# Expert lists built from two-byte one-hots, one decode for all heads, and attention products on array halves

## The chip, the cores and the metric

The kernel runs on one core of a Trainium2 chip. The core has a matrix engine (PE, whose weight loads are shown apart as PEld), a vector engine (DVE), an activation engine (ACT), a general engine (POOL) that here issues the gathers, and SP, which issues most other DMAs. The metric is the device time of one execution in microseconds (us). Before the change it is 3013.2 us, the median of three runs (3012.96 to 3013.81).

## The reference, cut to what matters

Two transformer blocks over 256 tokens of width 2048, all in float32. The first has a windowed grouped-query attention beside a linear recurrence, then a layer of 16,384 experts (`peer`); the second has two more attentions and a gated feed-forward. The change touches three places:

```python
# first block, attention: 16 query heads of 64, 4 key heads, a sink per head
s = jnp.einsum('bnqgrd,bnkgd->bngrqk', qb, kb) * (HEAD_DIM ** -0.5)
p = jnp.exp(s - m); p = p / (jnp.sum(p, -1, keepdims=True) + jnp.exp(sk - m))
o = jnp.einsum('bngrqk,bnkgd->bnqgrd', p, vb)

# peer: per token and head, 16 best of 128 row scores, 16 best of 128 column
# scores, then the 16 best of their 256 sums
v1, i1 = lax.top_k(s1, 16); v2, i2 = lax.top_k(s2, 16)
cand = (v1[..., :, None] + v2[..., None, :]).reshape(T, 8, 256)
cidx = (i1[..., :, None] * 128 + i2[..., None, :]).reshape(T, 8, 256)
sc, sel = lax.top_k(cand, 16)
eidx = jnp.take_along_axis(cidx, sel, axis=-1); gates = softmax(sc)
# per token: sum over its 128 picks of gate * gelu(x . u_emb[e]) * v_emb[e]

# second block, dense attention of 8 heads: 128 plain and 64 rotated columns,
# the rotated key shared by the heads
s = (einsum('bqhd,bkhd->bhqk', q_nope, k_nope)
     + einsum('bqhd,bkd->bhqk', q_rope, k_rope)) * scale
```

## The kernel before

Each dense product (`linear`) splits a 1 MB weight tile into a rounded part `whi` (ACT, L123) and a rest `wlo` (DVE, L124), and runs three products per 128x512 piece (PE, L134 to L136) for the two halves of the tokens, 24 for each tile. `whi` and `wlo` rotate over four half-tiles.

The expert layer goes in four steps. Scores come from `w_pq`. The *u phase* multiplies all 16,384 expert rows `u` (32 column groups, L113 loads them, L786 applies gelu, L797 writes the activations to a DRAM table `ag`). Beside it, at a lower priority, DVE finds and decodes the picks: `top16`, the 256 sums `cand` (L605), and per head three operations that turn a pick's place into a row and a column key (L626, L628, L630). Then the gates are spread over the experts by one-hot products (L658 to L674, PE L668), 64 steps in four groups; each group is written out to `ag` (L678) and reduced (L679) to a map of the experts in use. From the map, the *list* gives each used expert a lane and a block: 16 steps of eight columns, each with one-hots of the lane (`ln`, L744) and of the block (`b1`, L746; weighted in L749 on ACT and L750 on DVE) and eight 128x202 products that add up the list of expert numbers (PE, L753). Its end (L755 to L763) gives the index tiles `idv` and `idg`. The *v phase* then gathers rows of `v_emb` (tiles `raw` and `vraw`) and of `ag` (tile `vag`) by these indices (POOL, L130) and multiplies only the blocks that are used, 12 or 24 products each; L827 to L831 make the gated activations `vh`, `vhh` and `vhl`.

The first attention (`attn1`, eight units of four heads and 128 queries) has scores with 64 rows each (L444), queries and keys lying in the lower or upper 64 partitions as the head is even or odd; `softmax_out` transposes the probabilities (L423) and multiplies with the values (L429), two heads giving the lower and two the upper 64 output partitions. In the second block's dense attention each score is a 128-row product (L1110) and a 64-row one (L1111) into one bank.

All instructions are written in program order with priorities; a scheduler sets the order on each engine before the run, and each engine then runs its own queue in that order (PE, DVE, ACT, POOL, SP each one).

Of the kernel before, what the change touches and what calls it, by code (L numbers as in the profile page):

```python
# [12 lines left out]
F32 = mybir.dt.float32  # L13
# [8 lines left out]
P = 128  # L22
T = 256
# [33 lines left out]
def tile_kernel(ctx: ExitStack, tc: tile.TileContext, A, out):  # L57
# [354 lines left out]

    def softmax_out(s, l, nh, vget, oget):

        r = small([P, nh], f"smr{nh}")
        V.reciprocal(r, l)
        for h in range(nh):
            V.tensor_scalar(s[:, h, :], s[:, h, :], r[:, h:h + 1], None, op0=ALU.mult)
        for h in range(0, nh, 2):
            tp = bank("tp")  # L420
            for hh in range(2):
                for kk in range(2):
                    TE.transpose(tp[:, (2 * hh + kk) * P:(2 * hh + kk + 1) * P],  # L423
                                 s[:, h + hh, kk * P:(kk + 1) * P], ident)
            pT = mix[0].tile([P, 4, P], F32, tag="pT", name="pT", bufs=2)
            S.activation(pT, tp.rearrange("p (a t) -> p a t", a=4), AF.Copy)
            for hh in range(2):
                for kk in range(2):
                    TE.matmul(oget(h + hh), lhsT=vget(h + hh, kk), rhs=pT[:, 2 * hh + kk, :],  # L429
                              start=kk == 0, stop=kk == 1)  # L430

# [3 lines left out]
    def attn1(c, f, tt, qT):  # L435
# [3 lines left out]
        s = ap_.tile([P, 4, T], F32, tag="s1", name="s1", bufs=3)  # L439
        for e in range(2):  # L440
            ps = bank("sc")
            b = slice(e * 64, e * 64 + 64)
            for j in range(2):
                TE.matmul(ps[:, j * T:(j + 1) * T], lhsT=qT[b, 2 * f + j, tt * P:(tt + 1) * P],  # L444
                          rhs=kT[b, g, :], start=True, stop=True)
            V.tensor_tensor(s[:, 2 * e:2 * e + 2, :], ps.rearrange("p (a t) -> p a t", a=2),
                            maskb[:, tt, :].unsqueeze(1).to_broadcast([P, 2, T]), op=ALU.add)
# [6 lines left out]
        for h in range(4):  # L454
# [6 lines left out]
        softmax_out(s, l, 4, lambda h, kk: vsb[:, kk, g * 64:g * 64 + 64],  # L461
                    lambda h: ob[h // 2 * 64:h // 2 * 64 + 64, h % 2 * P:(h % 2 + 1) * P])
        sq = sqt()
# [130 lines left out]
    for tt in range(2):  # L594
# [6 lines left out]
        sc = rt.tile([P, 8, 16], F32, tag="rsc", name="rsc")  # L601
        sel = rt.tile([P, 8, 16], U32, tag="sel", name="sel")
        for h in range(8):
            cand = rt.tile([P, 16, 16], F32, tag="cand", name="cand", bufs=2)
            V.tensor_tensor(cand, v16[:, 2 * h, :].unsqueeze(2).to_broadcast([P, 16, 16]),  # L605
                            v16[:, 2 * h + 1, :].unsqueeze(1).to_broadcast([P, 16, 16]), op=ALU.add)
            top16(sc[:, h, :], sel[:, h, :], cand.rearrange("p a b -> p (a b)"), 256)

# [9 lines left out]
        for half, op, c in ((0, ALU.logical_shift_right, 4), (1, ALU.bitwise_and, 15)):  # L618
            ai = rt.tile([P, 8, 16], U32, tag="seli", name="seli", bufs=2)
            V.tensor_scalar(ai, sel, c, None, op0=op)  # L620
            af = rt.tile([P, 8, 16], F32, tag="self", name="self", bufs=2)
            V.tensor_copy(af, ai)
            kf = rt.tile([P, 8, 16], F32, tag=f"kf{half}", name="kf")
            for h in range(8):
                eq = rt.tile([P, 16, 16], F32, tag="eq", name="eq", bufs=2)
                V.tensor_tensor(eq, af[:, h, :].unsqueeze(2).to_broadcast([P, 16, 16]),  # L626
                                iota[:, 0:16].unsqueeze(1).to_broadcast([P, 16, 16]), op=ALU.is_equal)
                V.tensor_tensor(eq, eq, xf[:, 2 * h + half, :].unsqueeze(1).to_broadcast([P, 16, 16]),  # L628
                                op=ALU.mult)
                V.tensor_reduce(kf[:, h, :], eq, axis=AX.X, op=ALU.add)  # L630
            dec.append(kf)
# [20 lines left out]
    for c in range(4):  # L652
        gsb = gp.tile([P, P, 64], F32, tag="gsb", name="gsb", bufs=1)
        for t0 in range(0, 64, 4):
            t = 64 * c + t0
            io = iota.unsqueeze(1).to_broadcast([P, 4, P])
            oh = gp.tile([P, 4, P], F32R, tag="oh2", name="oh2", bufs=2)
            V.tensor_tensor(oh, io, i2T[:, t:t + 4].unsqueeze(2).to_broadcast([P, 4, P]), op=ALU.is_equal)  # L658
            o1 = gp.tile([P, 4, P], F32, tag="oh1", name="oh1", bufs=2)
            V.tensor_tensor(o1, io, i1T[:, t:t + 4].unsqueeze(2).to_broadcast([P, 4, P]), op=ALU.is_equal)  # L660
            og = gp.tile([P, 4, 2, P], F32R, tag="og", name="og", bufs=2)
            V.tensor_tensor(og[:, :, 1, :], o1, gT[:, t:t + 4].unsqueeze(2).to_broadcast([P, 4, P]), op=ALU.mult)
# [29 lines left out]
    V.tensor_copy(trib, tri)  # L692
    iota1 = kp.tile([P, P], F32, tag="iota1", name="iota1")
    V.tensor_scalar(iota1, iota, 1.0, None, op0=ALU.add)
# [36 lines left out]
    V.tensor_scalar(ti[:, 1:2, :], pli, 7, None, op0=ALU.logical_shift_right)  # L731
    lb = kt_("lb", 2)
    V.tensor_copy(lb, ti)
    lane, blk = lb[:, 0, :], lb[:, 1, :]

    ids2 = bank("x")[:, 0:2 * NL].rearrange("p (m b) -> p m b", m=2)
    J = 8

    def bc(x, j, n):
        return x[:, j:j + J].unsqueeze(2).to_broadcast([P, J, n])  # L740

    for j in range(0, P, J):
        ln = kp.tile([P, J, P], BF16, tag="ln", name="ln", bufs=2)
        V.tensor_tensor(ln, iota.unsqueeze(1).to_broadcast([P, J, P]), bc(lane, j, P), op=ALU.is_equal)  # L744
        b1 = kp.tile([P, J, NL], BF16, tag="b1", name="b1", bufs=2)
        V.tensor_tensor(b1, iota[:, 0:NL].unsqueeze(1).to_broadcast([P, J, NL]), bc(blk, j, NL), op=ALU.is_equal)  # L746
        bb = kp.tile([P, 2, J, NL], BF16, tag="bb2", name="bb2", bufs=2)
        with prompt():
            S.activation(bb[:, 0], b1, AF.Copy, scale=pidx[:, 0:1])  # L749
        V.tensor_tensor(bb[:, 1], b1, bc(iota1, j, NL), op=ALU.mult)  # L750
        with prompt():
            for i in range(J):
                TE.matmul(ids2, lhsT=ln[:, i, :], rhs=bb[:, :, i, :], start=j + i == 0, stop=j + i == P - 1)  # L753
    ids = kp.tile([P, 2, NL], F32, tag="ids", name="ids")
# [310 lines left out]
    kr = headnorm([kb[:, 0:64], kb[:, P:P + 64]], 1, 64, r12)  # L1065
    krT = mq.tile([P, 1, T], F32, tag="krT", name="krT")
    krd = []
    for tt in range(2):
# [4 lines left out]
        krd.append(k2)  # L1073
    trans(lambda tt, j: krd[tt].rearrange("p a d -> p (a d)"), 1, krT)

    gate(0)
# [21 lines left out]
    for h0 in (0, 4):  # L1098
        for tt in range(2):
# [4 lines left out]
            for e in range(2):  # L1104
                ps = bank("sc")
                b = slice(64 * e, 64 * e + 64)
# [174 lines left out]
```

## Time and profile before

| What | Value |
|---|---|
| Median of three runs | 3013.2 us |
| Profiled execution, its own time | 3017.87 us |
| Span of its trace, first to last instruction | 3016.0 us |
| PE busy | 2958.9 us, 98% |
| DVE busy | 2005.1 us, 66% |
| ACT busy | 1578.3 us, 52% |
| Mean granted PE clock | 0.993 |

Matmuls overlap each other in the engine, so one lasts 0.39 us in the trace while the next starts 0.23 us after it: distances between starts tell the pace, and a busy share near 100% says only that PE has no idle stretch. The u phase lies at about 430 to 1210 us, the list at 1143 to 1218 us, the v phase from 1235 us to about 1630 us. The first attention lies at 184 to 299 us, the dense attention's scores at 1980 to 2032 us.

### The profile page before, as it was taken

How to read it: one execution, taken by the hardware profiler on the slowest of the kernel's cores; microseconds unless marked ns; L12 is line 12 of the kernel's file. 1: busy time of each engine (PE TensorE's matmuls, PEld its weight loads, DVE VectorE, ACT ScalarE, POOL GpSimd, SP SyncE). 2: the span in 40 equal slices, each digit the busy share in tenths (PEclk: the TensorE clock that was granted, in tenths of full speed). 3: DMA queues.
4: the chain of work that ended last, by engine and by line, in shares of the span. 5: the costliest groups of instructions: out<-in, count | busy, mean ns of one | idle time of the engine just before them, and what ended most of it. 6: DMA issues, size and time to landing. Idle time of an engine off the chain costs nothing. (4 is left out here: it accounts for less than half of the span.)

```text
span 3016.0 us, 36313 instructions
## 1 busy us (share of the span) xinstructions
PE 2958.9 (98%) x13729; PEld 2437.0 (81%) x13729; DVE 2005.1 (66%) x2958; ACT 1578.3 (52%) x2221; POOL 270.7 (9%) x232
## 2 busy tenths in 40 slices
PE   9999999999999999699999999999999999999999
PEld 7887888887888878588887788878888888888887
DVE  6886689977778769577777666754655445445454
ACT  6754545565666655455556455544444444344443
POOL 0000000000000000677661000000000000000000
PEclk9999999999999999899999999999999999999999
DMA  6452546657576673788885555545655555555554
GB/s 227 157 182 98 198 175 202 219 190 243 197 250 199 235 246 118 268 337 315 332 319 206 174 178 189 201 151 202 236 190 181 196 184 192 196 193 184 195 188 161
DMA packets 197296, 626.26 MB, mean 208 GB/s; under 512 B 82816, under 2 KB 116224, under 8 KB 129792
## 3 DMA queue, kind: packets, MB, share of 16 engines
q1 hardware_dynamic: 139520, 477.33, 46.0%
q0 software_dynamic: 20784, 124.79, 11.1%
q10 hardware_dynamic: 36816, 21.81, 2.4%
q8 instruction: 108, 1.77, 0.2%
q14 instruction: 68, 0.56, 0.1%
HBM read 583.77 MB, written 40.11 MB: 207 GB/s over the span
## 5 line engine op out<-in xcount | busy, mean ns | idle before, releaser
L124 DVE TENSOR_TENSOR wlo<-raw,whi 128x1024 fp32r<-128x1024 f32 (+1 forms) x844 | 1026.5, 1221 | 705.2 <-ACT whi L123 683.9
L123 ACT ACTIVATE whi<-raw 128x1024 fp32r<-128x1024 f32 (+1 forms) x844 | 889.6, 1058 | 960.3 <-PE lin L136 823.8
L135 PE MATMUL lin<-wlo,x1th 128*128 128x512 f32 x1152 | 453.0, 393 | 8.5 <-DVE wlo L124 8.5
L136 PE MATMUL lin<-whi,x1tl 128*128 128x512 f32 x1152 | 452.6, 393 | 0.0
L134 PE MATMUL lin<-whi,x1th 128*128 128x512 f32 x1152 | 445.7, 395 | 0.4 <-ACT whi L123 0.4
L136 PE MATMUL lin<-whi,x3tl 128*128 128x512 f32 x704 | 274.9, 391 | 0.0
L135 PE MATMUL lin<-wlo,x3th 128*128 128x512 f32 x704 | 274.2, 389 | 0.0
L134 PE MATMUL lin<-whi,x3th 128*128 128x512 f32 x704 | 269.6, 390 | 0.0
L135 PEld LDWEIGHTS lin<-wlo,x1th 128*128 128x128 f32 x1152 | 217.5, 189 | 52.1 <-DVE wlo L124 10.2
L136 PEld LDWEIGHTS lin<-whi,x1tl 128*128 128x128 f32 x1152 | 217.3, 189 | 42.4
L134 PEld LDWEIGHTS lin<-whi,x1th 128*128 128x128 f32 x1152 | 217.1, 189 | 41.7 <-ACT whi L123 0.8
L135 PE MATMUL lin<-wlo,y1th 128*128 128x512 f32 x512 | 201.6, 394 | 0.8 <-DVE wlo L124 0.8
L134 PE MATMUL lin<-whi,y1th 128*128 128x512 f32 x512 | 200.2, 397 | 1.7 <-ACT y1th L160 1.2
L136 PE MATMUL lin<-whi,y1tl 128*128 128x512 f32 x512 | 199.5, 395 | 0.8 <-DVE y1tl L161 0.8
L124 DVE TENSOR_TENSOR wlo<-uraw,whi 128x1024 fp32r<-128x1024 f32 x128 | 155.8, 1221 | 51.6 <-ACT whi L123 50.9
L123 ACT ACTIVATE whi<-uraw 128x1024 fp32r<-128x1024 f32 x128 | 135.2, 1058 | 103.7 <-PE lin L136 101.4
L135 PEld LDWEIGHTS lin<-wlo,x3th 128*128 128x128 f32 x704 | 132.2, 188 | 27.2
L136 PEld LDWEIGHTS lin<-whi,x3tl 128*128 128x128 f32 x704 | 132.2, 188 | 27.1
L134 PEld LDWEIGHTS lin<-whi,x3th 128*128 128x128 f32 x704 | 132.2, 188 | 27.0
L130 POOL DMA_INDIRECT raw<-in_v_dram,idv x61 | 80.2, 1315 | 684.9 <-DVE idg L763 637.6
L130 POOL DMA_INDIRECT vag<-ag,idg x102 | 134.0, 1313 | 53.1 <-issue 27.4
L136 PE MATMUL lin<-whi,at 128*128 128x512 f32 x352 | 137.2, 390 | 0.0
(442 smaller groups left out, 5046.3 us busy)
## 6 DMA issues: line engine op xcount, KB each, us to landing
raw<-in_w_in_dram SPq DMA_DIRECT2D x91, 1024.0 KB, 4.8
raw<-in_w_gu_dram SPq DMA_DIRECT2D x88, 1024.0 KB, 4.8
uraw<-in_u_dram SPq DMA_DIRECT2D x64, 1024.0 KB, 4.8
raw<-in_u_dram SPq DMA_DIRECT2D x64, 1024.0 KB, 4.9
raw<-in_w_dn_dram SPq DMA_DIRECT2D x44, 1024.0 KB, 4.8
raw<-in_w_out_dram SPq DMA_DIRECT2D x16, 1024.0 KB, 4.8
raw<-in_w_pq_dram SPq DMA_DIRECT2D x16, 1024.0 KB, 4.8
ag<-actT ACTq DMA_DIRECT2D x64, 256.0 KB, 3.0
```

Source lines behind the costliest of these rows:

```text
L123: S.activation(h[:, q], r, AF.Copy)
L124: V.tensor_sub(l[:, q], r, h[:, q].bitcast(F32))
L130: G.indirect_dma_start(out=dst, out_offset=None, in_=src, in_offset=bass.IndirectOffsetOnAxis(ap=rows, axis=0))
L134: TE.matmul(ps, lhsT=xh, rhs=wh, start=start, stop=False)
L135: TE.matmul(ps, lhsT=xh, rhs=wl, start=False, stop=False)
L136: TE.matmul(ps, lhsT=xl, rhs=wh, start=False, stop=stop)
```

## The change

Four edits.

- The list's tiles are made in bfloat16 throughout, with the eight keys of a step innermost, so that a column of the one-hot for key `i` lies eight elements (16 bytes) from the next; a constant `iox` repeats the counter eight times. PE reads weights and moving columns with that step.
- Sums and decoded keys are made for all eight heads in one operation each (2048 elements a partition), in one shared buffer.
- The one-hot tiles `oh2` and `og` of the gates get a third buffer.
- In `attn1` the scores of the two array halves are issued in turn into two banks, and the value products of two head pairs in turn once both transposes are copied out. In the dense attention the rotated key is kept twice, each copy with zeros in the other 64 partitions (`krz`), and the product has 128 rows.

```diff
-    def softmax_out(s, l, nh, vget, oget):
+    def softmax_out(s, l, nh, vget, oget, pairs=False):
...
+            pTs.append(pT)
+            if pairs and h == 0:
+                continue
             for hh in range(2):
                 for kk in range(2):
-                    TE.matmul(oget(h + hh), lhsT=vget(h + hh, kk), rhs=pT[:, 2 * hh + kk, :],
-                              start=kk == 0, stop=kk == 1)
+                    for i, pT in enumerate(pTs if pairs else pTs[-1:]):
+                        hd = 2 * i + hh if pairs else h + hh
+                        TE.matmul(oget(hd), lhsT=vget(hd, kk), rhs=pT[:, 2 * hh + kk, :],
+                                  start=kk == 0, stop=kk == 1)
...
-        for e in range(2):
-            ps = bank("sc")
-            b = slice(e * 64, e * 64 + 64)
-            for j in range(2):
+        pss = [bank("sc"), bank("sc")]
+        for j in range(2):
+            for e, ps in enumerate(pss):
+                b = slice(e * 64, e * 64 + 64)
                 TE.matmul(ps[:, j * T:(j + 1) * T], lhsT=qT[b, 2 * f + j, tt * P:(tt + 1) * P],
                           rhs=kT[b, g, :], start=True, stop=True)
...
+        cand = rt.tile([P, 8, 16, 16], F32, tag="cand", name="cand", bufs=1)
+        V.tensor_tensor(cand, halfof(v16, 0, 3), halfof(v16, 1, 2), op=ALU.add)
         for h in range(8):
-            cand = rt.tile([P, 16, 16], F32, tag="cand", name="cand", bufs=2)
-            V.tensor_tensor(cand, v16[:, 2 * h, :].unsqueeze(2).to_broadcast([P, 16, 16]),
-                            v16[:, 2 * h + 1, :].unsqueeze(1).to_broadcast([P, 16, 16]), op=ALU.add)
...
-            for h in range(8):
-                eq = rt.tile([P, 16, 16], F32, tag="eq", name="eq", bufs=2)
...
+            eq = rt.tile([P, 8, 16, 16], F32, tag="cand", name="eq", bufs=1)
+            V.tensor_tensor(eq, af.unsqueeze(3).to_broadcast([P, 8, 16, 16]),
+                            iota[:, 0:16].unsqueeze(1).unsqueeze(1).to_broadcast([P, 8, 16, 16]), op=ALU.is_equal)
+            V.tensor_tensor(eq, eq, halfof(xf, half, 2), op=ALU.mult)
+            V.tensor_reduce(kf, eq, axis=AX.X, op=ALU.add)
...
-            oh = gp.tile([P, 4, P], F32R, tag="oh2", name="oh2", bufs=2)
+            oh = gp.tile([P, 4, P], F32R, tag="oh2", name="oh2", bufs=3)
...
-            og = gp.tile([P, 4, 2, P], F32R, tag="og", name="og", bufs=2)
+            og = gp.tile([P, 4, 2, P], F32R, tag="og", name="og", bufs=3)
...
-    iota1 = kp.tile([P, P], F32, tag="iota1", name="iota1")
+    iota1 = kp.tile([P, P], BF16, tag="iota1", name="iota1")
...
-    lb = kt_("lb", 2)
+    lb = kt_("lb", 2, BF16)
...
+    iox = kp.tile([P, P, J], BF16, tag="iox", name="iox")
+    V.tensor_copy(iox, iota.unsqueeze(2).to_broadcast([P, P, J]))
 
     def bc(x, j, n):
-        return x[:, j:j + J].unsqueeze(2).to_broadcast([P, J, n])
+        return x[:, j:j + J].unsqueeze(1).to_broadcast([P, n, J])
 
     for j in range(0, P, J):
-        ln = kp.tile([P, J, P], BF16, tag="ln", name="ln", bufs=2)
-        V.tensor_tensor(ln, iota.unsqueeze(1).to_broadcast([P, J, P]), bc(lane, j, P), op=ALU.is_equal)
-        b1 = kp.tile([P, J, NL], BF16, tag="b1", name="b1", bufs=2)
-        V.tensor_tensor(b1, iota[:, 0:NL].unsqueeze(1).to_broadcast([P, J, NL]), bc(blk, j, NL), op=ALU.is_equal)
-        bb = kp.tile([P, 2, J, NL], BF16, tag="bb2", name="bb2", bufs=2)
+        ln = kp.tile([P, P, J], BF16, tag="ln", name="ln", bufs=2)
+        V.tensor_tensor(ln, iox, bc(lane, j, P), op=ALU.is_equal)
+        b1 = kp.tile([P, NL, J], BF16, tag="b1", name="b1", bufs=2)
+        V.tensor_tensor(b1, iox[:, 0:NL, :], bc(blk, j, NL), op=ALU.is_equal)
+        bb = kp.tile([P, 2, NL, J], BF16, tag="bb2", name="bb2", bufs=2)
         with prompt():
             S.activation(bb[:, 0], b1, AF.Copy, scale=pidx[:, 0:1])
         V.tensor_tensor(bb[:, 1], b1, bc(iota1, j, NL), op=ALU.mult)
         with prompt():
             for i in range(J):
-                TE.matmul(ids2, lhsT=ln[:, i, :], rhs=bb[:, :, i, :], start=j + i == 0, stop=j + i == P - 1)
+                TE.matmul(ids2, lhsT=ln[:, :, i], rhs=bb[:, :, :, i], start=j + i == 0, stop=j + i == P - 1)
...
+    krz = mq.tile([P, 2, T], F32, tag="krz", name="krz")
+    G.memset(krz, 0.0)
+    for e in range(2):
+        b = slice(64 * e, 64 * e + 64)
+        V.tensor_copy(krz[b, e, :], krT[b, 0, :])
...
                     TE.matmul(o, lhsT=qT[:, h, t], rhs=kT[:, h, :], start=True, stop=False)
-                    TE.matmul(o, lhsT=qrT[b, h // 2, t], rhs=krT[b, 0, :], start=False, stop=True)
+                    TE.matmul(o, lhsT=qrT[:, h // 2, t], rhs=krz[:, e, :], start=False, stop=True)
```

The scheduler places instructions anew. On PE, the scores of the last of the eight attention units (even heads, then odd heads) stand like this in the kernel before, with products of the output projection and another unit's transposes between them:

```order
L444 MATMUL sc<-kT,qT 128x256 x2
L134 MATMUL lin<-whi,yah 128x512
L135 MATMUL lin<-wlo,yah 128x512
L136 MATMUL lin<-whi,yal 128x512
L134 MATMUL lin<-whi,yah 128x512
L135 MATMUL lin<-wlo,yah 128x512
L423 MATMUL tp<-ident,s_1947 128x128 x8
L136 MATMUL lin<-whi,yal 128x512
L134 MATMUL lin<-whi,yah 128x512
L444 MATMUL sc<-kT,qT 128x256 x2
```

And in the changed kernel, where L452 is the same line, L436 the value products and L425 the transposes:

```order
L452 MATMUL sc<-kT,qT 128x256 x4
L134 MATMUL lin<-whi,yah 128x512
L436 MATMUL ob<-pT,v 64x128 x8
L135 MATMUL lin<-wlo,yah 128x512
L136 MATMUL lin<-whi,yal 128x512
L425 MATMUL tp<-ident,s_2007 128x128 x8
```

The two halves of the unit now stand together. So they do in units 7 and 8; in unit 5 and 6 they meet in part (2 and 2, 3 and 1), in units 1, 2 and 4 they stood together before, and unit 3 keeps its order. The eight value products of a unit alternate between the two transposed tiles in all eight. On POOL, at the start of the v phase, the gathers stand like this before (`raw` and `vraw` are 1 MB of `v_emb` each, `vag` are rows of the table `ag`):

```order
L130 DMA raw<-in_v_dram,idv 128x2048 x3
L130 DMA vag<-ag,idg 128x256 x4
L130 DMA vag<-ag,idg 128x512 x2
L130 DMA vag<-ag,idg 128x256 x4
L130 DMA vraw<-in_v_dram,idv 128x2048 x2
L130 DMA raw<-in_v_dram,idv 128x2048
```

And in the changed kernel:

```order
L130 DMA raw<-in_v_dram,idv 128x2048 x3
L130 DMA vraw<-in_v_dram,idv 128x2048 x2
L130 DMA vag<-ag,idg 128x256 x4
L130 DMA vag<-ag,idg 128x512 x2
L130 DMA vag<-ag,idg 128x256 x4
L130 DMA raw<-in_v_dram,idv 128x2048
```

Two 1 MB gathers have moved ahead of the ten gathers of activations.

## Rows read from the trace of the kernel before

**Rows 1.** Page, first part: busy us, share, instructions.
```profile
PE 2958.9 (98%) x13729; PEld 2437.0 (81%) x13729; DVE 2005.1 (66%) x2958; ACT 1578.3 (52%) x2221; POOL 270.7 (9%) x232
```

**Rows 2.** Busy time by stretch; at the end PEclk, DMA share, GB/s.
```profile
250.00:280.00 30.00, 30.00 (x144) 21.75 (x144) 24.00 (x59) 17.42 (x49) 0.00 (x0) 1.00 0.31 106
280.00:300.00 20.00, 16.16 (x104) 12.08 (x103) 8.21 (x27) 7.23 (x16) 0.00 (x0) 1.00 0.07 19
...
300.00:600.00 300.00, 300.00 (x1420) 249.58 (x1419) 255.90 (x687) 157.55 (x206) 0.53 (x1) 1.00 0.58 200
1143.00:1210.30 67.30, 67.30 (x363) 54.92 (x361) 64.05 (x63) 36.33 (x41) 0.00 (x0) 1.00 0.29 94
```

**Rows 3.** Waits of PE: us in total, times, longest.
```profile
PE tp L134 <- ACT vhh L829: 19.0, 1, 19.0
PE lin L135 <- DVE wlo L124: 11.1, 8, 2.8
```

**Rows 4.** Timeline of PE, attention products: start, us, instruction, count.
```profile
184.68 1.14 PE L444 MATMUL sc<-kT,qT 64*128 64x256 f32 x8
...
251.98 1.13 PE L444 MATMUL sc<-kT,qT 64*128 64x256 f32 x4
...
203.50 1.58 PE L429 MATMUL ob<-pT,v 128*64 128x128 f32 x16
...
1786.48 1.95 PE L429 MATMUL ob<-pT,vd 128*128 128x128 f32 x16
```

**Rows 5.** Timeline of PE, scores of the second block's attentions.
```profile
1740.12 1.46 PE L1018 MATMUL sc<-kT,qT 128*128 128x256 f32 x6
...
2019.87 0.70 PE L1111 MATMUL sc<-krT,qrT 64*128 64x256 f32 x2
2020.50 0.70 PE L1110 MATMUL sc<-kT,qT 128*128 128x256 f32 x2
```

**Rows 6.** Groups by line: count, busy us, mean ns, idle before.
```profile
L1111 PE MATMUL sc<-krT,qrT 64*128 64x256 f32 x32 | 11.1, 428 | 0.0
```

**Rows 7.** Timeline of PE, one step of the list.
```profile
1153.98 0.88 PE L753 MATMUL x<-bb,ln 128*128 128x202 bf16 x8
```

**Rows 8.** Groups by line and shape of DVE: count, busy us, mean ns, idle.
```profile
L744 DVE TENSOR_TENSOR ln<-iota,lb 128x1024 bf16<-128x1024 f32 x16 | 19.5, 1220 | 4.4 <-PE x L753 4.2
L750 DVE TENSOR_TENSOR bb<-b,iota 128x808 bf16<-128x808 bf16 x16 | 15.9, 992 | 0.0
L626 DVE TENSOR_TENSOR eq<-self,iota 128x256 f32<-128x256 f32 x32 | 12.3, 415 | 0.0
...
L622 DVE CAST self<-seli 128x128 f32<-128x128 uint32 x4 | 0.9, 216 | 0.0
```

**Rows 9.** Timeline from the last u product to the v phase, all engines.
```profile
1210.48 1.58 PE L753 MATMUL x<-bb,ln 128*128 128x202 bf16 x16
...
1216.55 0.37 DVE L755 COPY ids<-x 128x202 f32<-128x202 f32 x1 [0.97 <-PE x L753]
1218.07 0.21 DVE L763 CAST idg<-idf 128x101 uint32<-128x101 f32 x1
...
1234.08 0.69 DVE L827 TENSOR_TENSOR vh<-vag 128x512 f32<-128x512 f32 x1 [3.24 <-DMA vag<-ag,idg]
1235.55 0.79 PE L134 MATMUL tp<-whi,vhh 128*128 128x512 f32 x1 [19.03 <-ACT vhh L829]
...
1242.48 2.01 ACT L123 ACTIVATE whi<-vraw 128x1024 fp32r<-128x1024 f32 x2 [2.76 <-DMA vraw<-in_v_dram,idv]
1243.59 0.73 PE L134 MATMUL tp<-whi,vhh 128*128 128x512 f32 x2 [2.56 <-ACT whi L123]
```

**Rows 10.** Busy time by stretch at the start of the v phase.
```profile
1227.00:1232.00 5.00, 0.00 (x0) 0.00 (x0) 2.36 (x2) 2.00 (x2) 3.86 (x4) 0.50 1.00 419
...
1241.00:1243.50 2.50, 0.04 (x1) 0.00 (x0) 0.00 (x0) 1.01 (x2) 1.89 (x3) 0.93 1.00 354
...
1246.00:1248.00 2.00, 2.00 (x7) 1.52 (x6) 2.00 (x2) 0.39 (x1) 1.88 (x1) 0.50 1.04 346
```

More of the change, by code (lines that the diff above doesn't have):

```diff
@@ L418, in softmax_out @@
             V.tensor_scalar(s[:, h, :], s[:, h, :], r[:, h:h + 1], None, op0=ALU.mult)
+        pTs = []
         for h in range(0, nh, 2):
@@ L439, in attn1 @@
         s = ap_.tile([P, 4, T], F32, tag="s1", name="s1", bufs=3)
-        for e in range(2):
-            ps = bank("sc")
-            b = slice(e * 64, e * 64 + 64)
-            for j in range(2):
+        pss = [bank("sc"), bank("sc")]
+        for j in range(2):
+            for e, ps in enumerate(pss):
+                b = slice(e * 64, e * 64 + 64)
                 TE.matmul(ps[:, j * T:(j + 1) * T], lhsT=qT[b, 2 * f + j, tt * P:(tt + 1) * P],
                           rhs=kT[b, g, :], start=True, stop=True)
+        for e, ps in enumerate(pss):
             V.tensor_tensor(s[:, 2 * e:2 * e + 2, :], ps.rearrange("p (a t) -> p a t", a=2),
@@ L461, in attn1 @@
         softmax_out(s, l, 4, lambda h, kk: vsb[:, kk, g * 64:g * 64 + 64],
-                    lambda h: ob[h // 2 * 64:h // 2 * 64 + 64, h % 2 * P:(h % 2 + 1) * P])
+                    lambda h: ob[h // 2 * 64:h // 2 * 64 + 64, h % 2 * P:(h % 2 + 1) * P], True)
         sq = sqt()
@@ L602, in tile_kernel, with halfof @@
         sel = rt.tile([P, 8, 16], U32, tag="sel", name="sel")
+        def halfof(x, half, axis):
+            x = x.rearrange("p (h s) a -> p h s a", s=2)[:, :, half, :]
+            return x.unsqueeze(axis).to_broadcast([P, 8, 16, 16])
+        cand = rt.tile([P, 8, 16, 16], F32, tag="cand", name="cand", bufs=1)
+        V.tensor_tensor(cand, halfof(v16, 0, 3), halfof(v16, 1, 2), op=ALU.add)
         for h in range(8):
-            cand = rt.tile([P, 16, 16], F32, tag="cand", name="cand", bufs=2)
-            V.tensor_tensor(cand, v16[:, 2 * h, :].unsqueeze(2).to_broadcast([P, 16, 16]),
-                            v16[:, 2 * h + 1, :].unsqueeze(1).to_broadcast([P, 16, 16]), op=ALU.add)
-            top16(sc[:, h, :], sel[:, h, :], cand.rearrange("p a b -> p (a b)"), 256)
+            top16(sc[:, h, :], sel[:, h, :], cand[:, h].rearrange("p a b -> p (a b)"), 256)
         g = rt.tile([P, 8, 16], F32, tag="gate", name="gate")
@@ L623, in tile_kernel @@
             kf = rt.tile([P, 8, 16], F32, tag=f"kf{half}", name="kf")
-            for h in range(8):
-                eq = rt.tile([P, 16, 16], F32, tag="eq", name="eq", bufs=2)
[L626 to L630, printed above, removed]
+            eq = rt.tile([P, 8, 16, 16], F32, tag="cand", name="eq", bufs=1)
[3 more added lines that the diff above has]
+            V.tensor_reduce(kf, eq, axis=AX.X, op=ALU.add)
             dec.append(kf)
@@ L1065, in tile_kernel @@
     kr = headnorm([kb[:, 0:64], kb[:, P:P + 64]], 1, 64, r12)
-    krT = mq.tile([P, 1, T], F32, tag="krT", name="krT")
+    krT = mp.tile([P, 512], F32, tag="hn", name="krT", bufs=3)[:, 0:T].rearrange("p (a t) -> p a t", a=1)
     krd = []
@@ L1105, in tile_kernel @@
                 ps = bank("sc")
-                b = slice(64 * e, 64 * e + 64)
                 for j in range(2):
```

## The prediction

> **What bounds the kernel now.** I read the page's busy shares first. PE is busy for 98% of the span, DVE for 66% [rows 1], so work taken from DVE is worth something only where PE waits for it. The list of PE's waits names few such places: one wait of 19.0 us for the gated activations at the start of the v phase, and 11.1 us in eight waits for `wlo` [rows 3]. Then the stretches: 300 to 600 us, where picks are found and decoded, is 100% PE; so is 1143 to 1210 us, with the list [rows 2]. What PE itself does there sets the time, and three of the four edits must be judged by PE's own pace. Last I read the timeline across the 19 us gap, where a chain of DVE, POOL and DMA sets the end.
>
> **Dense attention, rotated key with 128 rows.** Two starts of L1018 (128 rows throughout) are 0.22 us apart: six in 1.46 us [rows 5]. Where L1111 (64 rows) and L1110 (128 rows) alternate, two instructions take 0.63 us, from 2019.87 to 2020.50, against 0.43 us [rows 5]. So each change between 64 and 128 rows costs 0.20 us. The 32 instructions of L1111 [rows 6] are 16 pairs, each entered and left once: 32 changes, 6.4 us. A few pairs border on each other's halves, so I take 6.0 us off. PE works without a break there. The clearing of `krz` on POOL and two copies on DVE fall between the rotated key and its first use, one gate product of four weight tiles and more later, and cost nothing; if that cover were gone they would cost about 1 us.
>
> **First attention.** Eight score instructions of both halves last 1.14 us, four of one half 1.13 us [rows 4]. The two halves therefore already run side by side wherever their instructions stand together, whatever their order; issuing them in turn gives nothing by itself. What gains is that units 7 and 8 now stand together and units 5 and 6 partly: one half's four instructions at 0.22 us and its two changes at 0.20 us, 1.26 us, go in each of the first two, and the four instructions, some 0.85 us, in each of the others: 4.2 us in all. The 16 value products of a unit last 1.58 us; sixteen with 128 output columns last 1.95 us [rows 4]. So only a part overlaps now, since the two heads of one half come first. In turn, they should take half of 1.95, about 0.97 us: 0.6 us less for each of eight units, 4.8 us. In unit 2 the new order puts a transpose between them, which I count as a change each way, some 0.3 us given back.
>
> Not all of it reaches the end. Up to 250 us other products fill PE, so four units' value products count: 2.4 - 0.3 = 2.1 us. From 250 to 280 us PE has no gap but DVE is busy 24.0 of 30 us, and from 280 to 300 us PE is busy only 16.2 of 20 us [rows 2]: the softmax chain is close behind. Of the 2.4 + 4.2 = 6.6 us there I take half, 3.3 us. Value products now wait for both transposed tiles; queued behind them on PE are output products of the same stretch, and that wait is my reason for the half. Sum: 5.4 us off, from 2 to 9.
>
> **Sums, decode and one-hot buffers.** 32 comparisons of 256 elements cost 12.3 us, 415 ns each [rows 8]; L628, L630 and the sums add like amounts. From L744 and L750, DVE needs (1220 - 992)/(1024 - 808) = 1.06 ns an element and 0.14 us an instruction [rows 8]. Eight small ones become one of 2.3 us, about 13 us less on DVE. PE does not wait there [rows 2]: I take 0. The cover is the four half-tiles that DVE keeps ahead of PE. In the new order, at these prices, no run of DVE work between two `wlo` passes 3.6 us before the gates. The longest runs are those of four reductions of the map (L679), 2048 elements or 2.3 us each, 9 us; I take them for the source of most waits for `wlo` [rows 3], and they stay as they are. The third buffers move the gates, not PE's work. Without cover I allow 2 us either way.
>
> **The list, on DVE.** A step costs 1.22 + 0.99 + 0.99 = 3.2 us, 16 steps 51 us. Whether two-byte operands throughout go faster no row shows: L750, with one four-byte operand of three, goes at full length [rows 8]. But DVE has a faster pace: L622 converts 128 elements in 216 ns, where 0.14 + 128 x 1.06 ns would be 275 [rows 8]. That is about half the price an element. Ends: 51 us, or 0.68 + 0.57 + 0.57 = 1.82 us a step, 29 us. I take the lower, as the nearest row with nothing in its way. The Trainium skill ("VectorE: DVE Perf Modes", section "The perf-mode tier table (the rule you actually need)") gives `tensor_tensor` double speed when all operands are 16-bit in SBUF. L750 before agrees on the negative side; by this rule DVE's list is 29 us.
>
> **The list, on PE.** Here is the main doubt. Eight products of 202 columns last 0.88 us from first start to last end: 0.09 us apart [rows 7], 0.44 ns a column. All operands are contiguous in the kernel before, so no row shows what a 16-byte step costs. PE has one slower pace in the trace: 0.22 us for 256 columns of L1018, 0.84 ns a column [rows 5]; at that a product takes 0.17 us, 0.08 us more, and 128 of them 10.5 us more. The other end is no loss. The farthest row is DVE's pace, 1.06 ns: 0.21 us a product, 16 us more. I take 0.17 us, between the two. The Trainium skill ("SBUF — State Buffer", section "Door 1: The DMA port swizzle") says that SBUF is read in 16-byte lines, that full bandwidth needs two hits a line, and that a change of line at each access pays a penalty. Every column here is on a line of its own; no run yet shows a price, and the page speaks against this edit.
>
> Of the 16 steps, 12 stand ahead of the last u product, where PE has no gap (67.3 of 67.3 us [rows 2]): 12 x 8 x 0.08 = 7.9 us more. The last four stand behind it, as before. There the chain runs 1210.5 (PE) to 1218.3 us (`idg`) [rows 9], with DVE waiting for PE's use of the two `ln` buffers and PE for DVE in turn. With DVE at 1.82 us a step PE's own work is left: four steps at 1.36 us, eight transposes at half of the 1.95 us of sixteen like products [rows 4], and DVE's closing operations, 1.7 us from 1216.55 [rows 9] and a start-up of 0.3: 8.4 us, some 0.5 us more than the 7.8. With no loss on PE it would be 4 x 0.7 + 1.0 + 2.0 = 5.8 us, 1.9 us less with rounding.
>
> **The start of the v phase.** Two gathers of 1 MB now stand ahead of the activations on POOL's queue. At 419 GB/s [rows 10] their 2.1 MB take 5.0 us, so `vh` (1234.08) and the first product (1235.55) come 5.0 us later after `idg` [rows 9]; everything of the v phase is queued behind. But the next weights were waited for then: 2.6 us until 1243.59, `whi` from `vraw` at 1242.48 [rows 9]. They now lie ready. That stall also fell when the clock had just risen (0.93 at 1241 to 1243.5 us) and was followed by a stretch at the lower level (0.50 at 1246 to 1248) [rows 10], that is 1.2 GHz instead of 2.4 for about 4 us, 2 us lost. 5.0 - 2.6 - 2.0 = 0.4 more, which I round to 0; from -3 to +5.
>
> **Sum.** -6.0 - 5.4 + 7.9 + 0.5 + 0 = -3.0 us against the profiled execution's 3017.9 us (a span of 3016.0 and 1.9 around it): 3014.9 us. That execution is 4.7 us above the median of 3013.2; taken off, 3010.2 us.
>
> **Rivals.**
> - *Strides are free on PE.* The terms +7.9 and +0.5 become 0 and -1.9: -13.3 us, 2999.9 us. For it: DVE and PE share no row of a penalty. Against it: PE asks for a column every 0.44 ns, more than twice as often as any other engine here.
> - *The weight loads come out from under the products* (slower). Each list product has a load of 128 columns, hidden now in 0.09 us. If both go at the slower pace and one after the other, 0.17 + 0.11 us a product, that is 0.19 us more, 24 us in 128: -11.4 + 24 = +12.6 us, 3025.8 us. It decides from 0.14 us a product above now, where the sum passes +6. Against it: loads overlap products everywhere in the trace.
> - *DVE stays at full length.* From the first list product to the last u product the new order has 128 dense products (27 us at 300 us for 1420 [rows 2]) and 12 steps (16 us at the slow pace), 43 us of PE; DVE would have 12 steps at 3.2 us and 13 `wlo` at 1.22, 54 us. 11 us late, less the half-tiles it is ahead, at most four of 12 products, 10 us: between +1 and +11. At +6, 3016 us.
> - *The attention gives nothing* because softmax is next in line, the list as forecast: -6.0 + 8.4 = +2.4, 3015.6 us.
>
> **Chances.** A change of under 0.2%, 6 us, cannot be told from none. The forecast 0.45 (3005 to 3015), free strides 0.30, exposed loads 0.10, full-length DVE 0.07, no gain in attention 0.08. Faster: 0.28 of the first, nearly all of the second, a little of the rest, 0.45. Slower: all exposed loads and a part of the last two and of the first, 0.15. The same: 0.40. The range leaves out the best of the free strides (attention in full) and the worst of the exposed loads: 2996 to 3020 us.
>
> **What would show it.** In the new profile: starts of L766 0.17 us apart (0.09: free strides; 0.28: exposed loads); L757 at 0.68 us and not 1.22; L1128 and L1129 all 0.22 us apart; sixteen L436 in about 1.0 us; the first `vhh` product 24 us after the last list product, instead of 19, with no stall behind it. I am wrong if L766 keeps 0.09 us or PE waits long for L763.

## The result and the profile after

The changed kernel takes 3043.6 us (median of four runs, 3043.05 to 3045.17), the kernel before 3013.4: a ratio of 1.0101, 95% interval 1.0084 to 1.0119, 30 us slower. The forecast was 3010.2 us, the range ended at 3020. The profiled execution lasts 3044.1 us (span 3042.2), 26.2 us more than that of before, which took 4.5 us more than its kernel's median.

The page's first part for the changed kernel, as [rows 1]: busy us, share, instructions.

```profile
PE 2985.6 (98%) x13729; PEld 2446.6 (80%) x13729; DVE 1976.0 (65%) x2863; ACT 1579.3 (52%) x2221; POOL 270.0 (9%) x233
```

PE has as large a busy share as before and 26.7 us more of busy time for the same 13,729 instructions, so the time is in what they last. PE's timeline at the list, as [rows 7] (start, us, instruction, count; 16 of the 128 list products stand in one row):

```profile
1160.94 0.39 PE L134 MATMUL lin<-whi,x1th 128*128 128x512 f32 x1
1161.17 5.99 PE L766 MATMUL x<-bb,ln 128*128 128x202 bf16 x16
1166.67 0.92 PE L135 MATMUL lin<-wlo,x1th 128*128 128x512 f32 x1
...
1168.24 0.63 PE L135 MATMUL lin<-wlo,x1th 128*128 128x512 f32 x1
1168.67 0.63 PE L136 MATMUL lin<-whi,x1tl 128*128 128x512 f32 x1
...
1172.46 0.39 PE L134 MATMUL lin<-whi,x1th 128*128 128x512 f32 x1
```

One product lasts 0.54 us, so the starts are (5.99 - 0.54)/15 = 0.363 us apart, where the kernel before had 0.09 [rows 7]. And the dense products behind the batch are 0.43 us apart instead of 0.23, for five us: these products belong to the u phase and were not edited. Busy time by stretch around that batch shows why (columns as in [rows 2]: PE, PEld, DVE, ACT, POOL, granted clock, DMA share, GB/s):

```profile
1164.00:1165.00 1.00, 1.00 (x4) 0.44 (x3) 0.69 (x2) 0.64 (x1) 0.00 (x0) 1.00 0.30 123
1165.00:1166.60 1.60, 1.60 (x5) 0.58 (x4) 0.49 (x2) 0.33 (x1) 0.00 (x0) 0.52 0.00 0
1168.00:1169.00 1.00, 1.00 (x4) 0.81 (x3) 1.00 (x3) 0.17 (x1) 0.00 (x0) 0.50 0.00 0
1172.00:1174.90 2.90, 2.90 (x14) 2.25 (x12) 0.93 (x1) 0.85 (x1) 0.00 (x0) 1.00 0.00 0
```

Four us into the batch the granted clock falls to 0.50 (1.2 GHz instead of 2.4), although PE shows no idle time, and it rises again some five us after the dense products have come back. The list products themselves don't notice: their starts are 0.36 us apart on both sides of the fall. All eight batches last as long, 5.99 to 6.01 us. The clock falls in the first seven, for some shorter than here, and the eighth runs at 0.50 from its start.

DVE's list operations, by line and shape, as [rows 8] (count, busy us, mean ns, idle):

```profile
L757 DVE TENSOR_TENSOR ln<-iox,lb 128x1024 bf16<-128x1024 bf16 x16 | 11.1, 692 | 38.1 <-PE x L766 38.1
L763 DVE TENSOR_TENSOR bb<-b,iota 128x808 bf16<-128x808 bf16 x16 | 9.1, 572 | 0.0
```

DVE is faster, as forecast, and waits 38 us for PE's list products. The start of the v phase, all engines, as [rows 9]:

```profile
1252.26 0.21 DVE L776 CAST idg<-idf 128x101 uint32<-128x101 f32 x1
...
1272.97 0.69 DVE L840 TENSOR_TENSOR vh<-vag 128x512 f32<-128x512 f32 x1 [0.49 <-DMA vag<-ag,idg]
1274.38 0.79 PE L134 MATMUL tp<-whi,vhh 128*128 128x512 f32 x1 [23.68 <-ACT vhh L842]
```

And the attention products on PE, as [rows 4] and [rows 5]: sixteen value products of a unit, and scores of the dense attention, all with 128 rows.

```profile
202.92 1.09 PE L436 MATMUL ob<-pT,v 128*64 128x128 f32 x16
...
2013.03 0.59 PE L1129 MATMUL sc<-krz,qrT 128*128 128x256 f32 x2
2013.45 0.59 PE L1128 MATMUL sc<-kT,qT 128*128 128x256 f32 x2
```

Where the time went is read best from the start of the same dense product (the first, second and so on of PE's 128x512 products) in both traces. After minus before: -0.6 us ahead of the first attention (180 us), -6.3 us once the first attention is over (340 us), -10.8 before the list (1151 us), +26.7 at the last u product (1210.3 before, 1237.0 after), +38.8 at the first v product, +35.7 at the 200th v product, +32.2 before the dense attention's scores, +26.1 at the end.

### The profile page after: what moved, and what is told of

Its sections match the earlier page's. It is cut to its first block, busy times and chain, and to the rows that moved or that the text cites. A ratio compares the mean times of both kernels' runs of the same rounds, so it can differ in the third digit from the quotient of the medians.

```text
span 3042.2 us, 36236 instructions
## 1 busy us (share of the span) xinstructions
PE 2985.6 (98%) x13729; PEld 2446.6 (80%) x13729; DVE 1976.0 (65%) x2863; ACT 1579.3 (52%) x2221; POOL 270.0 (9%) x233
```

## The experiments

### Is it the list, and which operand?

The list of the kernel before in the changed kernel:

```diff
-        ln = kp.tile([P, P, J], BF16, ...); V.tensor_tensor(ln, iox, bc(lane, j, P), ...)
+        ln = kp.tile([P, J, P], BF16, ...); V.tensor_tensor(ln, iota..., bc(lane, j, P), ...)   # b1, bb alike
-                TE.matmul(ids2, lhsT=ln[:, :, i], rhs=bb[:, :, :, i], ...)
+                TE.matmul(ids2, lhsT=ln[:, i, :], rhs=bb[:, :, i, :], ...)
```

> The changed kernel with the list of the kernel before put back (float32 counter, index innermost, contiguous operands on PE); the attention products, the single decode and the third buffers stay. Theory A (the whole loss is the list's 16-byte step on PE: 128 products at 0.362 us instead of 0.088 are 35 us, and the low clock behind each batch some 9 more): list products 0.088 us apart, clock 1.00 over the list, and the rest of the change keeps what the new trace shows for it, 6 us in the first attention, 6 in the dense attention and up to 4 in the u phase: 2997 to 3002 us. Rival B (a part of the loss lies in the gathers' new order at the v phase or in the decode): 3003 us or more, with the first v product more than 19 us after the end of the list.

Measured: 3009.8 us against 3014.1, ratio 0.9986 (0.9976 to 0.9996), 4 us faster where A wanted 11 or more. Against the changed kernel it is 34 us faster, so the list's layout is where the loss is. Products are 0.09 us apart again, and the clock is at 1.00 up to 1202.9 us. For the rest, B's time holds but not its sign: the wait for `vhh` is 19.0 us as before, and yet PE's lead over the kernel before, 13 us at the end of the u phase, is 0.3 us at the first v product (1235.26 against 1235.55 [rows 9]). PE's and DVE's timelines in that run, before and behind the last u product (1197.0), up to the indices:

```profile
1192.82 0.88 PE L764 MATMUL x<-bb,ln 128*128 128x202 bf16 x8
...
1209.59 1.23 DVE L755 TENSOR_TENSOR ln<-iota,lb 128x1024 bf16<-128x1024 f32 x1
1210.72 1.00 DVE L757 TENSOR_TENSOR b<-iota,lb 128x808 bf16<-128x808 f32 x1
1211.63 1.01 DVE L761 TENSOR_TENSOR bb<-b,iota 128x808 bf16<-128x808 bf16 x1
1212.54 1.23 DVE L755 TENSOR_TENSOR ln<-iota,lb 128x1024 bf16<-128x1024 f32 x1
1213.68 1.01 DVE L761 TENSOR_TENSOR bb<-b,iota 128x808 bf16<-128x808 bf16 x1
...
1217.83 0.22 DVE L774 CAST idg<-idf 128x101 uint32<-128x101 f32 x1
...
1235.26 0.79 PE L134 MATMUL tp<-whi,vhh 128*128 128x512 f32 x1 [18.99 <-ACT vhh L840]
```

DVE works without a gap until the list's last step and PE waits 8.1 us for it in six waits: eight of the 16 list steps now stand behind the last u product, where the kernel before had four (10.6 us of PE's lead stand before the list; the rest is about what the four steps cost that PE still has to do). `idg` is ready when it was before [rows 9]. This asked for the decode alone (below).

The operands one at a time, first the moving columns and then the weights laid out contiguously for PE, each written with a step by the engine that makes it:

```diff
-        bb = kp.tile([P, 2, NL, J], BF16, ...)
+        bb = kp.tile([P, 2, J, NL], BF16, ...).rearrange("p m j n -> p m n j")
```

> The changed kernel, only that the moving operand bb is laid out with the blocks innermost, so PE reads its columns 2 bytes apart; DVE and ACT write it with a step. The weights ln keep their 16-byte step. Theory A1 (the price is the moving operand's): products no longer 0.362 us apart but at most as long as the weight load, 0.146 us, clock at 1.00 over the list, time 3000 to 3008 us. Rival A2 (the weight load with its step is what PE waits for): products stay above 0.3 us apart and the time stays near 3040 us.

```diff
-        ln = kp.tile([P, P, J], BF16, ...)
+        ln = kp.tile([P, J, P], BF16, ...).rearrange("p j n -> p n j")
```

> The changed kernel, only that the weights ln are laid out with the lanes innermost, so PE loads them contiguously; bb keeps its 16-byte step. Theory A1 (price in the moving operand): weight loads back to 95 ns, products still 0.36 us apart, 3042 to 3045 us. Rival A2 (price in the weight load): products 0.09 to 0.2 us apart, about 3000 to 3010 us. If both share it, in between.

PE's timeline, first with `bb`, then with `ln` contiguous; and in each the DVE group that writes with a step:

```profile
1159.96 0.93 PE L767 MATMUL x<-bb,ln 128*128 128x202 bf16 x8
...
L764 DVE TENSOR_TENSOR bb<-b,iota 128x808 bf16<-128x808 bf16 x16 | 62.3, 3919 | 0.0
```

```profile
1162.98 5.88 PE L767 MATMUL x<-bb,ln 128*128 128x202 bf16 x16
...
L758 DVE TENSOR_TENSOR ln<-iox,lb 128x1024 bf16<-128x1024 bf16 x16 | 76.2, 4766 | 3.4 <-PE x L767 3.4
```

A1 holds for the products: with contiguous moving columns eight take 0.93 us although each weight load still lasts 146 ns; with contiguous weights 16 take 5.88 us. The price is that of the moving operand. The forecast times missed: 3037.6 us (ratio 1.0078, 1.0061 to 1.0095) and 3054.9 us (1.0139, 1.0122 to 1.0156), and in both DVE now writes with a step, of 202 or 256 bytes, at 3.92 or 4.77 us instead of 0.57 or 0.69. In the first PE waits 23.5 us for that `bb` and 3.2 us for the half that ACT writes, in the second 5.7 us. PE's layout was paid for on DVE and ACT.

### What DVE's faster pace needs

```diff
+    io2 = kp.tile([P, P], BF16, ...); V.tensor_copy(io2, iota)
-        ln = kp.tile([P, P, J], ...); V.tensor_tensor(ln, iox, lane[:, j:j + J].unsqueeze(1)..., ...)
+        ln = kp.tile([P, J, P], ...); V.tensor_tensor(ln, io2..., lane[:, j:j + J].unsqueeze(2)..., ...)   # b1, bb alike
```

> The changed kernel with the index innermost as before, so all PE operands are contiguous, but counter, lanes and blocks in bfloat16, the key broadcast along the innermost axis. Theory D1 (DVE's faster pace needs only two-byte operands): the comparisons take 0.69 us as in the changed kernel instead of 1.22, the step's three operations 1.83 us instead of 3.2, and the time is 1 to 3 us below that of the kernel with the old list, 2995 to 3001 us. Rival D2 (the pace needs the operands to step through the innermost axis; a repeated value there costs it): 1.22 and 0.99 us as before, and the time is that of the old list within 1 us.

DVE's group for `ln`:

```profile
L757 DVE TENSOR_TENSOR ln<-io,lb 128x1024 bf16<-128x1024 bf16 x16 | 19.6, 1227 | 1.9 <-PE x L766 1.9
```

D2 holds: all operands have two bytes, and it is 1.23 us as before; 3009.8 us, ratio 0.9983 (0.9974 to 0.9993), the time of the run with the old list. A key repeated along the innermost axis costs the pace. The Trainium skill ("VectorE: DVE Perf Modes", section "What auto-detection actually checks") asks for a step of one element in every tensor, beside the two bytes; this row agrees.

### How the price depends on the step

Both needs can be met if two keys instead of eight lie innermost. The list's tiles get one more axis, `[P, J // K, P, K]`; K = 2 and 4 give steps of 4 and 8 bytes; the changed kernel with J = 16, all 16 keys innermost, gives 32:

```diff
-        ln = kp.tile([P, P, J], BF16, ...)          # b1, bb, iox alike
+        ln = kp.tile([P, J // K, P, K], BF16, ...)
-                TE.matmul(ids2, lhsT=ln[:, :, i], rhs=bb[:, :, :, i], ...)
+                TE.matmul(ids2, lhsT=ln[:, i // K, :, i % K], rhs=bb[:, :, i // K, :, i % K], ...)
```

> The changed kernel with the list's keys in groups of two: two keys innermost, then the index, then the groups. PE reads moving columns and weights with a step of 4 bytes instead of 16; the numbers of operations and elements are the same. Theory S1 (a moving column costs by the bytes it steps over, 0.362 us for 202 columns of 16 bytes, that is 0.11 ns a byte, and not less than the 0.44 ns of contiguous columns): products 0.09 us apart, clock at 1.00, the list's DVE operations still at 0.69 and 0.57 us if pairs are enough for DVE; with DVE's list 20 us shorter than in the run with the old list and PE free, 2995 to 3004 us. Rival S2 (any step that isn't contiguous costs the same): products 0.36 us apart and about 3043 us. Rival D2 (pairs are not enough for DVE's faster pace): products 0.09 us, DVE at 1.22 and 1.00 us, and about 3010 us as with the old list.

> The same with groups of four keys, a step of 8 bytes. Theory S1 (by the bytes stepped over): products 0.18 us apart, 12 us more on PE than at 0.09, a shorter stretch of low clock or none, 3003 to 3018 us. Rival S2 (one price for every step): 0.36 us and about 3043 us. Rival S3 (a threshold: full pace up to 8 bytes): 0.09 us and the time of the run with a step of 4 bytes.

> The changed kernel with 16 keys in a step instead of 8, all 16 innermost: 8 steps of 16 products, PE's step is 32 bytes instead of 16. Theory S1 (a moving column costs by the bytes it steps over): products 0.72 us apart and a time of 3085 us or more. Rival S4 (it costs by the 16-byte lines it touches, and a column of its own line is the most there is): products 0.36 us apart, as with a step of 16 bytes, and 3035 to 3055 us.

PE's timeline with a step of 4 bytes, and a DVE group; then with 8; then with 32:

```profile
1162.98 1.66 PE L770 MATMUL x<-bb,ln 128*128 128x202 bf16 x16
...
L761 DVE TENSOR_TENSOR ln<-iox,lb 128x1024 bf16<-128x1024 bf16 x16 | 11.0, 687 | 7.5 <-PE x L770 7.5
```

```profile
1161.17 3.12 PE L770 MATMUL x<-bb,ln 128*128 128x202 bf16 x16
```

```profile
1165.40 12.06 PE L766 MATMUL x<-bb,ln 128*128 128x202 bf16 x32
```

| Step of a moving column | 2 bytes | 4 | 8 | 16 | 32 |
|---|---|---|---|---|---|
| Start to start of a product (median), us | 0.089 | 0.093 | 0.184 | 0.363 | 0.371 |
| Columns in 16 bytes | 8 | 4 | 2 | 1 | 1 |

The run with 32 bytes took 3043.0 us, once. S1 holds up to 16 bytes, S4 from there on: 202 columns at 0.363 us are 1.8 ns for each 16 bytes entered, or 0.44 ns for a column if that is more. S2 and S3 are excluded by the 8-byte run, D2 by the 0.687 us that DVE takes with pairs. The Trainium skill ("SBUF — State Buffer", section "Door 1: The DMA port swizzle") names these lines of 16 bytes, and the 32-byte run agrees; but it holds two hits a line to be enough, and with two (8 bytes) PE has half its pace. Four are needed here. The same passage of the Trainium skill lets eight two-byte elements be stepped over at no cost, which the prediction passed over; the changed kernel has exactly that step, and its products are four times as far apart as contiguous ones.

With 4 bytes the whole change gives 3000.6 us, ratio 0.9949 (0.9932 to 0.9965), with 8 bytes 3011.1 us (0.9987, 0.9977 to 0.9997). PE's order is that of the changed kernel, so the first is its twin without the price. In the stretch from the first list product to the end of the last, start to start:

| | changed kernel | step of 4 bytes | difference |
|---|---|---|---|
| 128 list products, us | 45.2 | 12.0 | 33.2 |
| 128 dense products, us | 41.1 | 29.8 | 11.3 |
| 16 transposes, us | 3.2 | 1.7 | 1.6 |
| stretch, us | 89.5 | 43.5 | 46.0 |

The clock is in the second and third row for the most part: 50 of the dense products are over 0.35 us apart in the changed kernel, none at 4 bytes. Busy time by stretch in the runs with 4 and with 8 bytes:

```profile
1170.00:1180.00 10.00, 10.00 (x68) 8.58 (x67) 7.43 (x12) 6.18 (x9) 0.00 (x0) 1.00 0.01 2
```

```profile
1170.00:1180.00 10.00, 10.00 (x50) 7.33 (x49) 5.83 (x9) 4.22 (x6) 0.00 (x0) 1.00 0.01 2
```

Even at 0.184 us a product the clock stays at 1.00 from the first list product to the last. That the slow batches bring it down is thus shown by their removal; what exactly the chip looks at isn't.

### The other edits by themselves

The attention edits alone, then the decode alone, then the third buffers alone, each its hunks of the diff applied to the kernel before:

```diff
-        softmax_out(s, l, 4, ..., lambda h: ob[...])
+        softmax_out(s, l, 4, ..., lambda h: ob[...], True)          # and scores in turn, krz
```

> The kernel before with the edits to both attentions alone; list, decode and one-hot buffers as before. In PE's order the gates and the list stand where they stood. Theory A (PE sets the time in both stretches, and what DVE does up to the list moves with PE): the 6.3 us of the first attention and the 6.1 us of the dense attention both reach the end, 3000 to 3003 us. Rival B (a chain that doesn't move with PE hides the first, as it did in the run with the old list): 3006 to 3009 us.

```diff
-            cand = rt.tile([P, 16, 16], F32, tag="cand", name="cand", bufs=2)
+        cand = rt.tile([P, 8, 16, 16], F32, tag="cand", name="cand", bufs=1)   # eq alike
```

> The kernel before with the sums and the decode for all heads at once, nothing else. In PE's order the last gate product moves from behind 4049 to behind 4122 dense products and the first list product from behind 4311 to behind 4394 (the last u product is number 4512), 83 products of 0.227 us, 19 us later. Theory A (DVE's list, at 3.2 us a step, then ends after PE's u phase and sets the start of the v phase): the wait for the gated activations starts earlier for PE, the list ends 4 to 8 us later than before, 3016 to 3021 us. Rival B (the decode's 13 us of DVE time saved make up for it): 3010 to 3014 us.

```diff
-            oh = gp.tile([P, 4, P], F32R, tag="oh2", name="oh2", bufs=2)   # og alike
+            oh = gp.tile([P, 4, P], F32R, tag="oh2", name="oh2", bufs=3)
```

> The kernel before with the third buffer of the two one-hot tiles and nothing else. In PE's order gates and list stay where they were, to a few products. Theory A (the buffers are off every chain): within 2 us of the kernel before. Rival B (they, not the decode, take away the waits for wlo in the u phase): 3 to 5 us faster.

The attention edits give 3003.0 us, ratio 0.9958 (0.9942 to 0.9975): A, both gains reach the end. Without the decode, list and `idg` (1209.42) move with PE. The buffers give 3016.7 against 3016.4, ratio 1.0000 (0.9990 to 1.0009): A. PE's waits for `wlo` in the run with the decode alone, then in that with the buffers alone (11.1 us before [rows 3]):

```profile
PE lin L135 <- DVE wlo L124: 7.3, 8, 1.7
...
PE lin L135 <- DVE wlo L124: 10.9, 8, 2.7
```

So it is the decode that shortens these waits, and not the buffers (B). Yet alone it is slower, 3022.3 against 3016.0, ratio 1.0023 (1.0013 to 1.0033): A, 1 us above its range of times. Its trace, the last list products and the index tile:

```profile
1212.09 1.53 PE L754 MATMUL x<-bb,ln 128*128 128x202 bf16 x8 [2.49 <-DVE bb L751]
1214.14 1.53 PE L754 MATMUL x<-bb,ln 128*128 128x202 bf16 x8 [0.52 <-DVE bb L751]
1218.00 1.53 PE L754 MATMUL x<-bb,ln 128*128 128x202 bf16 x8 [2.34 <-DVE bb L751]
1220.05 1.53 PE L754 MATMUL x<-bb,ln 128*128 128x202 bf16 x8 [0.52 <-DVE bb L751]
1223.13 0.21 DVE L764 CAST idg<-idf 128x101 uint32<-128x101 f32 x1
```

PE is 8 us ahead of the kernel before at the end of the u phase (5.3 us of it before the list begins), and `idg` comes 5.1 us later (1223.13 against 1218.07 [rows 9]): the wide operations move the gates and with them map and list back in the scheduler's order, and DVE's half of the list, at 3.2 us a step, is left for the end. Why the scheduler places the gates later wasn't tried.

### Can the list be early?

In the kernel before with the attention edits and the list at 4 bytes, without the decode and the third buffers, all list steps stand ahead of the last u product:

> The kernel before with the edits to both attentions and the list in two-byte operands with groups of two keys (step of 4 bytes); sums, decode and one-hot buffers as before. In PE's order all 16 list steps now stand ahead of dense product 4470 of the 4512 of the u phase. On POOL six 1 MB gathers of rows stand ahead of the activations' gathers. Theory A (the list's end, not PE, sets the start of the v phase, so an earlier list shortens the 25 us between last u product and first v product): the list ends about 1191 us, 10 us before the last u product; first v product 8 to 14 us after the last u product; 2988 to 2996 us. Rival B (the row gathers can't start while the u phase holds the buffers, or their 6 MB, 15 us, push the activations back): about 25 us from u to v as before, 3001 to 3004 us, the time of the run with the attention edits alone.

It gives 3001.1 us, ratio 0.9960 (0.9946 to 0.9974), no better than the attention edits alone (0.9958): B. So DVE's faster list is worth nothing where the list isn't late, and 9 to 11 us behind the decode edit (3000.6 us, ratio 0.9949, at 4 bytes; 3009.8 us, 0.9986, with the old list). The list's indices are ready at 1198.2, 8 us before the last u product, but the first v product comes 24 us after it. POOL's timeline (the wait before each in brackets):

```profile
1211.02 0.94 POOL L130 DMA_INDIRECT raw<-in_v_dram,idv  x1 [6.45 <-DVE wlo L124]
...
1218.44 0.94 POOL L130 DMA_INDIRECT vraw<-in_v_dram,idv  x1 [6.48 <-DVE wlo L124]
1221.38 0.95 POOL L130 DMA_INDIRECT vag<-ag,idg  x1 [2.01 <-DMA ag<-actT]
```

Two row gathers wait for buffers ahead of the activations. The last run ties these two to an index copy made after the first gated activations:

```diff
+        if i == 5:
...
+            V.scalar_tensor_tensor(idw, got[order[0]][0][0][:, 0:NL].bitcast(F32), 0.0, idv, op0=ALU.mult, op1=ALU.add)
-        vh, vl = wtile(VE, rows=idv[:, b:b + 1], raw=raw)
+        vh, vl = wtile(VE, rows=(idw if i in (5, 6) else idv)[:, b:b + 1], raw=raw)
```

> The run with attention edits and 4-byte list, in which two row gathers stood ahead of the activations' gathers on POOL and each waited 6.5 us for a buffer; here the row gathers of the sixth and seventh block take their indices from a copy that is made once the first gated activations are there, so the queue reads five rows gathers, the activations, then those two. Theory A (those two waits are what kept the first v product at 24 us after the last u product): activations gathered as soon as the last group of u is written, first v product 12 to 16 us after the last u product, 2988 to 2996 us. Rival B (the row gathers that were put back are then late and PE waits for them instead): 2997 to 3003 us, with a wait for whi of 5 us or more behind the first blocks.

```profile
1216.38 0.95 POOL L130 DMA_INDIRECT vag<-ag,idg  x1 [14.36 <-DMA ag<-actT]
...
1224.37 0.80 PE L134 MATMUL tp<-whi,vhh 128*128 128x512 f32 x1 [14.72 <-ACT vhh L844]
```

3000.9 us, ratio 0.9950 (0.9934 to 0.9967): no difference that these runs can tell. A's time is missed although its two waits are gone, and its sign too: the first v product comes 21 us after the last u product (1203.24), not 12 to 16. What stands between them is no longer the list: gelu and transposes, then the last part of the activations' table, issued at 1210.32 and waited for until 1216.38 with five row gathers of 1 MB on the queues, then gather and gating. Against the run before, the first v product is 5.1 us earlier (1224.37 against 1229.51). Of that 2.6 us stood there already at the last u product (1203.24 against 1205.81), and by the 200th v product 2.2 us are left. In between PE waits for a weight tile and then runs some products at the lower clock (second line: stretch, as in [rows 2]):

```profile
1262.04 0.79 PE L134 MATMUL tp<-whi,vhh 128*128 128x512 f32 x1 [2.18 <-issue]
1262.10:1264.00 1.90, 1.90 (x5) 1.51 (x6) 1.90 (x2) 0.84 (x1) 1.59 (x2) 0.50 0.90 285
```

That is a wait of B's kind, less than half as long as B had it; whether the two gathers that were put back cause it isn't shown. The best versions, this one and the changed kernel with a step of 4 bytes, are equal within their intervals.

## Why the prediction was wrong, step by step

- **The list on PE: wrong, the step that failed.** I took 0.17 us a product, between no loss and DVE's pace of 0.21, "the farthest row". It is 0.363, outside both ends. The rows of before held only contiguous columns and the pace of other engines on other work, and neither bounds a step that nobody took. The term of +8.4 us (7.9 and 0.5) is 33 us by itself in the stretch table.
- **The clock: missing from the sum.** Slow products let the granted clock fall without any idle PE, and that costs the dense products and transposes between them up to 13 us more (11.3 and 1.6 in the table). I had looked at the clock only where PE waits.
- **Exposed weight loads** was the slower rival, at 3025.8 us. Its mechanism is excluded: loads with the step last 146 ns and hide; the columns are the price. Free strides, the faster rival, are excluded by the 0.363 us; at 4 bytes, where the price is gone, the gain is 15 us, and that rival had 13.
- **Sums and decode: 0 forecast, +7 us alone.** "PE does not wait there" was true of the decode's own stretch, but the edit moves the list 83 dense products, 19 us, back in PE's order (73 in the changed kernel). I had counted the 128 dense products that are left behind it, and used them only for a rival in which DVE's list stays slow. That is the run with the old list: it eats 13 us of PE's lead. In the changed kernel DVE waits 38 us for PE's slow list, so there it doesn't show. And I left the waits for `wlo` unchanged; they fell from 11.1 to 7.3 us, most of the 4.5 us that PE gains between 340 us and the list, and the run with the decode alone has the same 7.3.
- **Third buffers: 0, right.**
- **DVE's list: right.** 0.69 and 0.57 us, where 0.68 and 0.57 were forecast; it waits for PE, so it is worth nothing here.
- **Dense attention: right.** -6.1 us (from +32.2 to +26.1) for -6.0.
- **First attention: right in size, in part by luck.** -5.7 us in the trace for -5.4 (0.6 of the 6.3 stand ahead of it); sixteen value products take 1.09 us, 0.97 forecast, 1.58 before [rows 4]. But the parts were off both ways: up to 244 us three units' value products give 0.9 us, where 0.6 us a unit was counted, and of the 5.9 us gained from there to 276 us only 1.1 are given back, where half of 6.6 was taken off for the softmax chain. The two attention terms together are the 12 to 13 us of the run with these edits alone.
- **Start of the v phase: right.** First product 23.7 us after the list (24 forecast), the stall behind it gone: 4.7 us lost and 3.1 regained by the 200th product. A further 3.5 us come back later in the v phase and right behind it. Between the same products the run with the buffers alone, whose median is that of the kernel before, is 3.8 us shorter than the trace of before: two executions differ there by as much without this change, and the 3.5 us are likely a part of the 4.5 us by which the profiled execution before lay above its median.

With the measured price in place of mine, the sum is -6.1 - 6.3 - 4.5 (u phase) + 46 (stretch, against its twin) + 4.7 - 3.1 - 3.5 (v phase) = +27 us, against 26.2 between the two profiled executions. All terms but the 46 are read from these two traces, so the agreement tests that term alone. Without the price the same change is 15 us faster than the kernel before.

## What to carry to other kernels

A layout has two readers: choose the innermost axis for the engine that writes it and for PE's moving operand together, and look for the small group that serves both (here two keys, 4 bytes) before moving a whole axis. A price that no row shows is not bounded by rows of other engines: ask what the wildest end would do, or measure it. And an edit on an engine that nobody waits for can still move what is issued behind it; follow in the order where the next chain lands.

## What the chip showed that was not expected

- PE's moving columns cost 1.8 ns for each 16 bytes entered, at 1.2 as at 2.4 GHz: 0.363 us for 202 columns at either clock. Weights with the same step cost nothing that could be seen (146 ns a load, yet products start 0.091 us apart at the median, with contiguous columns).
- The granted clock fell to 0.50 while PE was busy without a break, 3 to 5 us into a batch of slow products, and rose again 2.5 to 5 us into the dense ones behind it (in the six batches of the u phase).
- DVE writes two-byte elements 202 or 256 bytes apart at an estimated 4.5 to 4.7 ns each ((3919 - 140)/808 and (4766 - 140)/1024, with the prediction's 0.14 us an instruction), eight to nine times its price with two keys innermost ((687 - 140)/1024 = 0.53 ns).
